# P4's bases loaded by quarters into the result tiles, and P7 begun with the two row pairs that P6 ended on

## The chip, the cores and the metric

One core of one Trainium2 chip. The metric is the device time of one execution in microseconds, the median of three runs for the kernel before.

## The reference

A soft mixture of experts: every token's output is the sum over all eight experts of that expert's matrix product, weighted by the router's softmax.

```python
batch, seq, hidden, n_experts, expert_hidden = 16, 512, 512, 8, 2048
probs = softmax(router_logits)                       # over the 8 experts
for e in range(n_experts):
    output += probs[:, :, e:e+1] * np.matmul(x, expert_weights[e])
```

As one product it is (8192 tokens) x (8 experts x 512) x (2048 columns): the left operand is x times a probability, the right operand is all the expert weights.

## The kernel before, in words

The product is cut in halves in all three directions and made by seven products instead of eight, twice over (Strassen's scheme in the form with seven products, an outer level P1 to P7 and an inner level of seven steps), and in some stages a third time. Rows are taken in 16 row pairs q; pair q has the row blocks 2q and 2q+1 of 256 tokens. Column half 0 or 1 has 1024 columns, of which a step takes 512.

An outer product r of pair q is `product(r, q)`. It has a left operand (`Left`, made by VectorE, DVE in the profile, from a block of x, a block of probabilities and for some products a kept operand), a right operand (`Right`, sums of weights), a *base* that is added to its result, and a sink that stores the result. Its seven inner steps run in the order `STEPS = (1, 5, 6, 2, 7, 3, 4)` on TensorE (PE), eight matmuls of 128x512 each. Every product gives four result tiles of 128x512 in f32, called (0,0), (1,1), (0,1) and (1,0) after row half and column half (`INNER`), 256 KB each. Steps 1, 5, 6 and 4 are the first that touch the bases (0,0), (1,1), (0,1) and (1,0); steps 2, 7, 3 and 4 are the last, after which the result is stored.

Work goes in *stages*, mostly of two products whose steps alternate. The order of the outer products is: P1 and P2, then P5 and P6 together, then eight stages of P7, eight of P4, and P3. P6's operand (its two halves `t[0]`, `t[1]`) is kept: `keep_z` stores it to `z_dram[q]`, and P7 and P3 read it back through a `ZBlock` of 1 MB. P7's base is P6's stored result, read back from the output; P4's base is P7's. P7's results are plain stores; P4's and P3's are stores that accumulate in DRAM, into (row block 2q+1, columns 0) for P4.

P4's stages are made "by thirds": `by_thirds` replaces steps 1 and 5 of both products by 14 short groups of matmuls of 128x256 (four slots), and the five other steps follow, two slots each; so a P4 stage has 14 slots, as every stage of two products has. `Thirds.make` lets DVE write four sums into one tile of the pool `w` per stage (line 538).

What sets the order: every engine runs its instructions in the order that the kernel wrote down. Loads go through SyncE's queue (`sp`, SP in the profile), weight loads through ScalarE's (ACT, which also copies results, lines 611, 624, 823 to 837), stores and casts through GpSimd's (`pool`, POOL, line 121). DVE's work beside the evacuations stands in a queue of tasks with assumed costs (`later`, `need`). `at(stage, slot, ...)` hangs a load on a slot of a stage. `start_loads` issues the loads of the stage after next.

Pools and what waits for them:

- `w`, 15 tiles of 8 KB per partition: all weights, the sums of `Thirds`, the parts of the next products' weights (`by_parts`), z loads, and the bases of the odd pair of each stage.
- `h`, 12 tiles of 2 KB per partition: results, and bases loaded one quarter at a time.
- `z`, 8 tiles: operands.

The base of an even pair is a `Base`: four loads of 256 KB into tiles of `h`. The base of an odd pair is a `WideBase`: one load of 1 MB into a tile of `w`, called `base` in the profile. In both cases the result is made in the base's own place, so a quarter's tile becomes free when its own store has landed, and the wide one when the last of its four stores has:

```python
base = self.base(tn) if first else o[tn]
if first:
    o[tn] = half() if self.apart else base
```

P6's last two stages are (P6 of 14, P5 of 15) and, alone, P6 of 15. P7 began with pairs 0 and 1; the loads for it were hung by hand on slots of those two stages, one operand in two halves (`begin_half`), and DVE's work for the second stage of P7 was held back to slot 4 (`wait_for[k7] = 4`).

Of the kernel before, what the change touches and what calls it, by code (L numbers as in the profile page):

```python
# [31 lines left out]
def kernel(  # L32
# [20 lines left out]
    NH = EH // 2  # L53
# [63 lines left out]
    def sp(o, i):  # L117
        note(nc.sync.dma_start(out=o, in_=i))
# [15 lines left out]
    def new_w():  # L134
        return wpool.tile([P, K8, NB], f16, name="w", tag="w")

    def new_u():
        return zpool.tile([P, K8, HQ], f16, name="u", tag="u", bufs=1)
# [355 lines left out]
    class ZBlock:  # L494
# [8 lines left out]
            self.t = [t[:, 0], t[:, 1]]  # L503
            sp(t, z_dram[self.q].rearrange("p (h k) t -> p h k t", h=2))

        def begin_half(self, k):
            if k == 0:
                t = new_u()
                self.t = [t, None]
            else:  # L510
                t = self.t[1] = new_w().rearrange("p k (two t) -> p (k two) t", two=2)[:, ds(0, K8)]
            sp(t, z_dram[self.q][:, ds(k * K8, K8), :])

        def finish(self):
            pass

# [145 lines left out]
            sp(t, self.source)  # L662
            self.t = {(i, n): t[:, i, n] for i in range(2) for n in range(2)}

    def base_of(q, odd):
        if q % 2:
            return WideBase(out_f[ds((2 * q + odd) * HQ, HQ), ds(NH, NH)]
                            .rearrange("(t p) (n m) -> p t n m", t=2, n=2))
        return Base(lambda tn: out_rows(q, odd, 1, tn))

    INNER = ((0, 0), (1, 1), (0, 1), (1, 0))

# [21 lines left out]
    def left_of(r, q, fresh=True):  # L694
        a, b = 2 * q, 2 * q + 1
        if r == 1:
            pt = PBlock(a, P1, xp1[q - 2][1] if q in (2, 3) else None)
            if q in (2, 3):
                xs[a] = XBlock(a, xp1[q - 2][0])
            return Left(xblock(a), pt), [xblock(a), pt]  # L700
        if r in (2, 4):
            h, pt = (a, PBlock(a, P2)) if r == 2 else (b, PBlock(b, P2))
            return Left(xblock(h), pt), [xblock(h), pt]
        if r == 5:
            pt = PBlock(b, PQ)
            return Left(xblock(b), pt), [xblock(b), pt]
        if r == 6:
            pt = PBlock(a, P1)
            return Left(xblock(a), pt, of=lefts[5, q]), [xblock(a), pt]
        h = a if r == 3 else b  # L710
        pt, kept_z = PBlock(h, P2), ZBlock(q)
        return Left(xblock(h), pt, kept=kept_z), [xblock(h), pt, kept_z]

    def kept_rows(q):
# [1 line left out]

    def product(r, q, **how):
        left, loads = left_of(r, q)
        lefts[r, q] = left
        p = None  # L720
        if r == 1:
            def sink(tn, o):
                pool(kept_rows(q)(tn), o)
            p = Product(right[1], left, sink)
        elif r == 2:
            if q >= QK:
                base = products[1, q].o.__getitem__
            else:
                base = bases[2, q] = Base(kept_rows(q))
            p = Product(right[2], left, to_out(q, 0, 0), base)  # L730
        elif r == 5:
            bases[6, q] = m1 = Base(kept_rows(q))
            m1.task = {}

            p = Product(right[5], left, to_out(q, 1, 0))
        elif r == 6:
            m1 = bases[6, q]

            def base(tn):
                need(m1.task[tn])  # L740
                return m1.t[tn]
            p = Product(right[6], left, to_out(q, 0, 1), base)
        elif r == 7:
            base = bases[7, q] = base_of(q, 0)
            p = Product(right[7], left, to_out(q, 1, 1), base)
        elif r == 4:
            base = bases[4, q] = base_of(q, 1)
            p = Product(right[4], left, to_out(q, 1, 0, accum_op=ADD), base)
        else:
            p = Product(right[3], left, to_out(q, 0, 1, accum_op=ADD), **how)  # L750
        p.loads = loads
        products[r, q] = p
        return p
# [144 lines left out]
    k6 = add(product(6, 15))  # L898
    ks = {}
    for r in (7, 4):  # L900
        for q in range(0, 16, 2):
            xs.clear()
            ks.setdefault(r, add(product(r, q), product(r, q + 1)))
    k7, k4 = ks[7], ks[4]
# [21 lines left out]
            at(*where, lambda q=q, tn=tn: joined(q, tn))  # L926
    def base_at(stage, slot, r, q, *tn):
        at(stage, slot, lambda: bases[r, q].fetch(*tn))
    for r, first in ((7, k7), (4, k4)):
        for q in range(0, 16, 2):  # L930
            k = first + q // 2
            for slot, tn in zip((1, 2, 3, 5) if k == k7 else (4, 6, 8, 10), INNER):
                base_at(k - 1, slot, r, q, tn)
            base_at(k - 1, 2 if k == k7 else 7, r, q + 1)


    def wedge(kn, e):
# [212 lines left out]
        at(k - 1, half_way, lambda keep_z=keep_z: keep_z(0))  # L1150
        at(k, 5 if q < 15 else 3, lambda keep_z=keep_z: keep_z(1))

    def load_z(stage, slot, r, q, *half):
        load = products[r, q].loads[-1]
        load.by_hook = True
        at(stage, slot, lambda: load.begin_half(*half) if half else load.begin())
    third_of = {4: {}, 3: {}}
    third_made = {4: [], 3: []}

    def make_third(stage, slot, r, p):  # L1160
        def make():
            third_of[r][p] = third_sums(right[r].w[p])
        at(stage, slot, lambda: third_made[r].append(later(2.76, make)))
    load_z(k6 - 1, 0, 7, 0)
    load_z(k6 - 1, 4, 7, 1, 0)
    load_z(k6, 0, 7, 1, 1)
    load_z(k6, 4, 7, 2)
    load_z(k6, 5, 7, 3)
    at(k6 - 1, 9, lambda: queue_left(lefts[7, 0]))
    wait_for[k7] = 4  # L1170
    make_third(k4 - 1, 7, 4, 1)
    make_third(k4 - 1, 9, 4, 5)
    load_z(k3 - 1, 0, 3, 0)
# [91 lines left out]
```

## Time and profile before

| what | value |
|---|---|
| runs | 1396.3 us median of 3 (1396.05 to 1398.36) |
| profiled execution | 1394.54 us, of which 1392.8 us are the span from the first to the last instruction |
| PE busy | 1364.2 us, 98% of the span |
| DVE busy | 1118.3 us, 80% |
| ACT, POOL busy | 227.7 us, 410.8 us |
| mean granted TensorE clock | 0.994 |
| DMA | 392.63 MB, mean 282 GB/s |

The profile's page adds up one profiled execution. Busy time is that of an engine's own instructions; the idle time before an instruction is put down to what ended it. "A <- B" in the view of waits reads: A waited for B, with the total, the number of times and the longest. In the chain of waits each row is start, duration, and what the end of the kernel hung on at that moment. In the timeline of one engine, rows that follow each other are merged, and what stands in square brackets is the idle time before the row. In the view of stretches a row has the stretch and its length, then for each engine the busy time and the number of instructions, then clock, DMA share and GB/s. Times count from the span's start.

### The profile page before, as it was taken

To read this page: it belongs to the slowest core of one execution; us is meant where nothing else is said; L and a number is where in the kernel's file an instruction comes from. 1 tells how busy PE (TensorE), PEld (TensorE's weight loads), DVE (VectorE), ACT (ScalarE), POOL (GpSimd) and SP (SyncE) were. 2 spreads that over 40 slices of the span, in tenths; PEclk is the share of its full clock that TensorE was granted. 3 is DMA by queue.
4 is the path that set the end of the run, shared out by engine and by line. 5 is a ranking of instruction groups with operands and counts; after the bars stand their busy time and mean duration, and the time that the engine had idled before them with its cause. 6 is when DMAs were issued, how large, how long until landed. Compare 5 with 4: busy or idle time off the path is not lost.

```text
span 1392.8 us, 18695 instructions
## 1 busy us (share of the span) xinstructions
PE 1364.2 (98%) x6798; PEld 664.2 (48%) x6798; DVE 1118.3 (80%) x1386; ACT 227.7 (16%) x453; POOL 410.8 (29%) x652
## 2 busy tenths in 40 slices
PE   9999999999999999999999989999999888999998
PEld 4555444444444444444444434444555454455554
DVE  7877667679789887978887778889877877988884
ACT  3232111100011111111111000000121111133331
POOL 3223233321222433333331112221333332223231
PEclk9999999999999999999999999999999999999999
DMA  9998989999899999999999999997999999999976
GB/s 185 226 241 226 218 265 239 266 281 390 263 291 284 341 329 289 330 281 316 290 313 320 409 372 394 307 350 294 327 227 275 239 293 262 330 297 255 223 105 128
DMA packets 198077, 392.63 MB, mean 282 GB/s; under 512 B 53472, under 2 KB 87520, under 8 KB 190304
## 3 DMA queue, kind: packets, MB, share of 16 engines
q0 software_dynamic: 88688, 185.12, 55.1%
q1 hardware_dynamic: 105264, 177.87, 39.7%
q10 hardware_dynamic: 4032, 28.44, 5.2%
q8 instruction: 53, 0.87, 0.2%
q14 instruction: 40, 0.33, 0.1%
HBM read 245.40 MB, written 173.21 MB: 301 GB/s over the span
## 4 chain that ended last, share of the span: by engine, by line
PE 86%; DMA 7%; issue 3%; DVE 2%; POOL 1%; ACT 0%; ACTq 0%; POOLq 0%; DVEq 0%; SPq 0%
PE ps L130 65%; PE pt L130 21%; DMA out_dram<-base 2%; DMA base<-out_dram 1%; DMA h<-out_dram 1%; POOL out_dram L121 1%; DMA w<-in_expert_weights_dram 1%; DMA xT<-x 1%; DMA w<-wd 1%; DVE z L107 1%; DVE w L107 0%; DVE h L107 0%; DVE ps L107 0%; POOL w L121 0%; POOL wd L121 0%
## 5 line engine op out<-in xcount | busy, mean ns | idle before, releaser
L130 PE MATMUL ps<-w,z 128*128 128x512 f16 (+1 forms) x3760 | 825.4, 376 | 12.6 <-DVE h L107 10.3
L130 PEld LDWEIGHTS <-z 128*128 128x128 f16 x5280 | 517.8, 98 | 601.5 <-issue 21.8
L121 POOL DMA_DIRECT2D out_dram<-h x316 | 203.5, 652 | 671.7 <-ACT h L624 282.5
L130 PE MATMUL pt<-w,z 128*128 128x512 f16 (+1 forms) x1520 | 323.0, 360 | 1.8 <-DVE ps L107 1.3
L107 DVE TENSOR_TENSOR z<-xT,pT 128x2048 f16<-128x2048 f16 x220 | 266.3, 1217 | 3.6 <-DMA xT<-xs 3.6
L107 DVE TENSOR_TENSOR h<-ps,h 128x512 f32<-128x512 f32 x226 | 154.7, 687 | 114.2 <-PE ps L130 107.3
L130 PE MATMUL ps<-w,d 128*128 128x512 f16 x880 | 202.4, 383 | 8.6 <-DVE ps L107 8.6
L130 PEld LDWEIGHTS <-d 128*128 128x128 f16 x880 | 86.6, 98 | 110.8 <-issue 12.1
L107 DVE TENSOR_TENSOR z<-z,d 128x2048 f16<-128x2048 f16 x110 | 132.3, 1217 | 0.0
L107 DVE TENSOR_TENSOR w<-w 128x1024 f16<-128x1024 f16 (+2 forms) x116 | 116.3, 1016 | 4.3 <-DMA w<-wd 2.6
L611 ACT COPY h<-ps 128x512 f32<-128x512 f32 x90 | 52.7, 586 | 363.9 <-PE ps L130 343.2
L107 DVE TENSOR_TENSOR h<-pt,h 128x512 f32<-128x512 f32 x109 | 74.9, 687 | 36.1 <-PE pt L130 28.5
L624 ACT COPY h<-ps 128x512 f32<-128x512 f32 x48 | 28.1, 586 | 356.7 <-PE ps L130 289.9
L107 DVE TENSOR_TENSOR z<-z,w 128x2048 f16<-128x2048 f16 x63 | 77.2, 1225 | 2.5 <-DMA w<-z 0.4
L107 DVE TENSOR_TENSOR d<-z 128x1024 f16<-128x1024 f16 x110 | 74.6, 684 | 0.7
L121 POOL DMA_DIRECT2D out_dram<-base x64 | 47.2, 738 | 62.7 <-DVE base L107 41.7
L121 POOL DMA_DIRECT2D wd<-w x86 | 50.1, 603 | 49.3 <-DVE w L107 29.2
L121 POOL DMA_DIRECT2D w<-in_expert_weights_dram x65 | 48.3, 754 | 49.9 <-DMA wd<-w 30.1
L107 DVE TENSOR_TENSOR ps<-ps,h 128x512 f32<-128x512 f32 (+1 forms) x68 | 42.1, 620 | 24.9 <-PE ps L130 15.7
L130 PEld LDWEIGHTS <-w 128*128 128x128 f16 x528 | 49.1, 98 | 7.8 <-DMA w<-in_x_dram 1.3
L107 DVE TENSOR_TENSOR base<-ps,base 128x512 f32<-128x512 f32 x64 | 43.8, 684 | 9.3 <-PE ps L130 9.3
L121 POOL DMA_DIRECT2D kept<-h x56 | 30.8, 550 | 68.0 <-ACT h L611 35.4
(80 smaller groups left out, 491.0 us busy)
## 6 DMA issues: line engine op xcount, KB each, us to landing
out_dram<-h POOLq DMA_DIRECT2D x316, 256.0 KB, 7.4
w<-z SPq DMA_DIRECT2D x31, 1024.0 KB, 11.9
pT<-p_dram SPq DMA_DIRECT2D x108, 256.0 KB, 9.4
w<-wd ACTq DMA_DIRECT2D x27, 1024.0 KB, 10.2
h<-kept SPq DMA_DIRECT2D x100, 256.0 KB, 7.2
wd<-w POOLq DMA_DIRECT2D x72, 256.0 KB, 8.0
xT<-x SPq DMA_DIRECT2D x71, 256.0 KB, 10.0
w<-in_expert_weights_dram POOLq DMA_DIRECT2D x35, 512.0 KB, 10.0
```

The lines of the kernel that those rows point to most:

```text
L107: dve(nc.vector.tensor_tensor(out=o, in0=a, in1=b, op=op))
L121: note(nc.gpsimd.dma_start(out=o, in_=i, **how))
L130: note(nc.tensor.matmul(ps, z, w, start=start, stop=stop, skip_group_check=True))
L611: act(nc.scalar.copy(o[TN[p]], b if p == 2 else x))
L624: act(nc.scalar.copy(o[tn], b))
```

## The change

For P4, the base of both pairs is now loaded by quarters into tiles of `h`, where the results are then made; no base of P4 lies in `w` any more. The eight quarter loads of a stage hang on slots 8, 10 and 12 of the stage before and on slot 3 of the stage itself.

P7 begins with pairs 14 and 15. Their bases are P6's results, taken from the tiles where they were made, and their kept operands are P6's operands, taken from their `z` tiles; neither is loaded. Pairs 0 to 13 follow. The hand-hung loads of operands before P7, `begin_half` and `wait_for[k7]` are gone; z loads go out with the other loads of their stage, and P7's bases for pairs 0 to 13 hang on slots 4, 6, 8, 10 and 7 of the stage before.

```diff
-    def base_of(q, odd):
+    def base_of(q):
         if q % 2:
-            return WideBase(out_f[ds((2 * q + odd) * HQ, HQ), ds(NH, NH)]
+            return WideBase(out_f[ds(2 * q * HQ, HQ), ds(NH, NH)]
                             .rearrange("(t p) (n m) -> p t n m", t=2, n=2))
-        return Base(lambda tn: out_rows(q, odd, 1, tn))
+        return Base(lambda tn: out_rows(q, 0, 1, tn))
...
-        pt, kept_z = PBlock(h, P2), ZBlock(q)
+        pt = PBlock(h, P2)
+        if r == 7 and q >= 14:
+            return Left(xblock(h), pt, kept=lefts[6, q]), [xblock(h), pt]
+        kept_z = ZBlock(q)
...
-            base = bases[7, q] = base_of(q, 0)
+            base = bases[7, q] = base_of(q) if q < 14 else products[6, q].o.__getitem__
...
-            base = bases[4, q] = base_of(q, 1)
+            base = bases[4, q] = Base(lambda tn: out_rows(q, 1, 1, tn))
...
-        for q in range(0, 16, 2):
+        for q in ((14, *range(0, 14, 2)) if r == 7 else range(0, 16, 2)):
...
-    for r, first in ((7, k7), (4, k4)):
-        for q in range(0, 16, 2):
-            k = first + q // 2
-            for slot, tn in zip((1, 2, 3, 5) if k == k7 else (4, 6, 8, 10), INNER):
-                base_at(k - 1, slot, r, q, tn)
-            base_at(k - 1, 2 if k == k7 else 7, r, q + 1)
+    for q in range(0, 14, 2):
+        k = k7 + 1 + q // 2
+        for slot, tn in zip((4, 6, 8, 10), INNER):
+            base_at(k - 1, slot, 7, q, tn)
+        base_at(k - 1, 7, 7, q + 1)
+    for q in range(16):
+        k = k4 + q // 2
+        for slot, tn in zip((8, 10, 12, 17), INNER):
+            base_at(k - 1 + slot // 14, slot % 14, 4, q, tn)
...
-    load_z(k6 - 1, 0, 7, 0)
-    load_z(k6 - 1, 4, 7, 1, 0)
-    load_z(k6, 0, 7, 1, 1)
-    load_z(k6, 4, 7, 2)
-    load_z(k6, 5, 7, 3)
-    at(k6 - 1, 9, lambda: queue_left(lefts[7, 0]))
-    wait_for[k7] = 4
+    at(k6 - 1, 5, lambda: queue_left(lefts[7, 14]))
```

More of the change, by code (lines that the diff above doesn't have):

```diff
@@ L504, in begin @@
             sp(t, z_dram[self.q].rearrange("p (h k) t -> p h k t", h=2))
[L506 to L512, printed above, removed]
         def finish(self):
@@ L1151, with load_z @@
         at(k, 5 if q < 15 else 3, lambda keep_z=keep_z: keep_z(1))
-    def load_z(stage, slot, r, q, *half):
+    def load_z(stage, slot, r, q):
         load = products[r, q].loads[-1]
         load.by_hook = True
-        at(stage, slot, lambda: load.begin_half(*half) if half else load.begin())
+        at(stage, slot, load.begin)
     third_of = {4: {}, 3: {}}
```

## The prediction

> **What bounds the kernel now.** I read the page first, then PE's waits, then the chain of waits, PE's timeline and a table of the P4 stages.
>
> ```profile
> PE 1364.2 (98%) x6798; PEld 664.2 (48%) x6798; DVE 1118.3 (80%) x1386; ACT 227.7 (16%) x453; POOL 410.8 (29%) x652
> L107 DVE TENSOR_TENSOR h<-ps,h 128x512 f32<-128x512 f32 x226 | 154.7, 687 | 114.2 <-PE ps L130 107.3
> ```
>
> ```profile
> PE ps L130 <- DVE h L107: 10.3, 4, 5.4
> PE ps L130 <- DVE ps L107: 8.6, 3, 4.0
> ```
>
> PE is the bound: 28.6 us of the 1392.8 us span are not PE's. The change leaves PE's instructions as they are, in number and shape, so all that it can win is idle time, and time in which PE runs slowly after a wait. PE's large waits are seven, all for DVE's evacuations of PSUM banks: 18.9 us. They stand in two places, the start of P7 and P4.
>
> The start of P7, first in the chain, then on PE:
>
> ```profile
> 769.03 10.01 DMA w<-wd
> 779.11 14.24 DMA h<-out_dram
> 793.37 12.35 DMA xT<-x
> 805.79 19.39 DMA base<-out_dram
> ```
>
> ```profile
> 797.53 1.89 PE L130 MATMUL ps<-w,d 128*128 128x512 f16 x8 [0.92 <-DVE ps L107]
> ...
> 820.50 1.89 PE L130 MATMUL ps<-w,d 128*128 128x512 f16 x8
> 826.05 3.46 PE L130 MATMUL ps<-w,d 128*128 128x512 f16 x8 [3.66 <-DVE ps L107]
> ```
>
> For 56 us the chain is one load after the other on SP's queue, each issued as the one before lands. The wide base that goes out at 805.79 lands 19.39 us later, at 825.18; PE wanted its evacuation at 822.4, waits 3.66 us, and then needs 3.46 us for eight matmuls that take 1.89 us elsewhere, 1.57 us more.
>
> P4, one row for each of its eight stages (stretch and length, then busy us of PE, PEld, DVE, ACT, POOL with their instructions, clock, DMA share, GB/s):
>
> ```profile
> 988.20:1011.58 23.38, 23.38 (x138) 13.29 (x137) 20.27 (x29) 4.09 (x10) 9.74 (x14) 1.00 1.10 309
> 1011.58:1036.14 24.56, 23.61 (x137) 13.31 (x136) 17.74 (x27) 4.09 (x10) 6.27 (x9) 1.00 0.93 240
> 1036.14:1060.96 24.82, 23.54 (x137) 13.30 (x136) 22.00 (x33) 4.09 (x10) 13.73 (x19) 1.00 1.09 235
> 1060.96:1092.70 31.74, 26.32 (x137) 13.91 (x136) 21.78 (x31) 4.09 (x10) 9.70 (x12) 0.89 1.00 247
> 1092.70:1116.08 23.38, 23.38 (x137) 13.31 (x136) 21.55 (x31) 4.09 (x10) 9.72 (x14) 1.00 1.10 273
> 1116.08:1144.86 28.78, 25.23 (x137) 13.74 (x136) 20.24 (x29) 4.09 (x10) 10.05 (x13) 0.94 1.08 309
> 1144.86:1168.24 23.38, 23.38 (x137) 13.33 (x136) 20.43 (x31) 4.09 (x10) 9.77 (x14) 1.00 1.08 241
> 1168.24:1199.20 30.96, 26.94 (x145) 14.53 (x144) 22.15 (x31) 3.92 (x10) 7.24 (x9) 0.94 1.02 321
> ```
>
> A stage without a wait takes 23.38 us. Stages two to seven are over that by 1.18, 1.44, 8.36, 0, 5.40 and 0: 16.38 us. Why, for the largest:
>
> ```profile
> DVE w L107 <- DMA out_dram<-base: 16.6, 2, 9.2
> ```
>
> ```profile
> 1069.19 13.71 DMA out_dram<-base
> 1086.52 6.35 PE ps L130 x16
> ```
>
> DVE stands still before it writes the sums of `Thirds` into a tile of `w`: the tile it gets was a wide base, and the last accumulating store out of it needs 13.71 us to land. DVE goes in order, so every evacuation behind it is late, and PE with it. The stage's last wait is another one: in the eighth stage a weight load for P3 waits on ACT's queue for the last store of a wide base (9.05 us), ACT's copies stand behind it, then DVE, then PE:
>
> ```profile
> 1169.50 9.05 DMA out_dram<-base
> 1180.27 19.11 PE ps L130 x80
> ```
>
> ```profile
> 1180.27 3.05 PE L130 MATMUL ps<-w,d 128*128 128x512 f16 x8 [4.02 <-DVE ps L107]
> ```
>
> 4.02 us idle and 3.05 - 1.89 = 1.16 us slow: 5.18 us.
>
> **How long stores and loads take** beside P4's work (the table of DMA issues, 985 to 1200 us; KB each, median us to landing):
>
> ```profile
> out_dram<-h POOLq DMA_DIRECT2D x34, 256.0 KB, 10.5
> out_dram<-base POOLq DMA_DIRECT2D x33, 256.0 KB, 10.1
> base<-out_dram SPq DMA_DIRECT2D x7, 1024.0 KB, 15.5
> w<-wd ACTq DMA_DIRECT2D x7, 1024.0 KB, 12.4
> h<-out_dram SPq DMA_DIRECT2D x26, 256.0 KB, 12.8
> ```
>
> Two pairs of quarters issued alone, at 1036 and 1091 us, then a store in a stage with parts of P3's weights (1052 us) and those of a calm one (1145 to 1169 us):
>
> ```profile
> h<-out_dram SPq DMA_DIRECT2D x2, 256.0 KB, 9.4
> ```
>
> ```profile
> h<-out_dram SPq DMA_DIRECT2D x2, 256.0 KB, 12.7
> ```
>
> ```profile
> out_dram<-h POOLq DMA_DIRECT2D x1, 256.0 KB, 12.4
> ```
>
> ```profile
> out_dram<-h POOLq DMA_DIRECT2D x5, 256.0 KB, 7.0
> ```
>
> The steps themselves, in the P4 stage that starts at 1144.86: step 6 of both products, then the four others:
>
> ```profile
> 1150.97 3.62 PE L130 MATMUL ps<-w,d 128*128 128x512 f16 x16
> 1154.43 13.98 PE L130 MATMUL ps<-w,z 128*128 128x512 f16 x64
> ```
>
> The first row starts 3.46 us ahead of the second: 1.73 us for a step of one product.
>
> **The start of P7, part by part.** The first stage (pairs 14, 15) loads no base and no z: 4 MB of loads leave SP's queue before it, so nothing stands between P6 and P7 but DVE's work, whose instructions are the same. The 0.92 us go. The second stage's loads (z of pairs 0, 1, xT, pT) move ahead, past P6's last loads of kept results on SP; POOL's stores keep their order. The wide base of pair 1 keeps its hook, slot 7 of the first stage, and its need, the third slot of the next stage; what it no longer has ahead of it is the backlog of the chain above. From its issue at 805.79 to PE's need at 822.4 it had 16.6 us; with the 15.5 us of the wide bases' row and 0.69 us for the evacuation that is just enough, and it is issued earlier where the queue before it is free. So the 3.66 and 1.57 us go too: 0.92 + 3.66 + 1.57 = 6.15 us. What could be late in their place: P7's results of pair 15 are written into tiles out of which P6's stores must have landed. (1,1) is the tightest, with P6's steps 3 and 4 and P7's steps 1 and 5 of two products in between, 1.73 x 2 + 3.46 x 2 = 10.4 us, less 0.69 us for the evacuation and about one for the issue. The nearest rows are P4's stores, 7.0 us where it is calm and 10.5 us at the median; I take nothing, and at worst the 2 us by which the slower one misses.
>
> **P4, part by part.** No base lies in `w`, so no sums of `Thirds` wait for an accumulating store: the 16.38 us go. What takes their place is a wait for `h`. Two products now hold eight tiles of its 12, so only two pairs of quarters of the next stage can be loaded ahead; the third, base (0,1), gets the tiles of (0,0), whose accumulating stores start in the middle of the stage. SP's in-order queue holds that load until the store has landed (behind it: xT and pT of two stages on, not urgent). The time that it has:
>
> ```profile
> 1157.24 0.88 POOL L121 DMA_DIRECT2D out_dram<-h x1 [0.48 <-ACT h L624]
> ```
>
> In the stage from 1144.86 the thirds take 6.11 us, step 6 of both products 3.46 us, and the first (0,0) is stored at 12.38 us. DVE adds base (0,1) after step 6 of the first product in the next stage, 23.38 + 6.11 + 1.73 = 31.22 us. That leaves 18.84 us for a store to land, a load to be issued (0.5 us) and to land. DVE is busy 20.77 us per stage (the eight rows' 166.16 us), so it can idle 2.61 us before the stage grows; PE itself waits later, at step 7, which needs the same bank 3.46 us after step 6 of the second product begins.
>
> Bounds per hand-over between stages (there are seven): calm, 7.0 + 0.5 + 9.4 = 16.9 us, no wait; at the medians 10.5 + 0.5 + 12.8 = 23.8 us, DVE idles 4.96 us and the stage grows by 2.35 us, 16.5 us over seven. I take the load as the mean of the two lone pairs, 11.05 us, since it is issued when SP's earlier loads have landed. In three stages, those with weight parts, the store takes 12.4 us: 23.95 us, growth 23.95 - 18.84 - 2.61 = 2.5 us each. In the other four, 7.0 + 0.5 + 11.05 = 18.55 us, nothing. Sum 7.5 us. The other quarters have more time: (1,0) follows the stores of (1,1) and is wanted only at the stage's end. Splitting moves no more bytes; SP issues 8 loads per stage where it issued 5, off the path.
>
> The eighth stage's 5.18 us: the tile that the P3 weights wait for no longer hangs on a base's store, but ACT's loads share the stretch with SP's late quarters and the first z load of P3, and a load held on ACT's queue again holds the copies behind it. Nothing in the trace prices that; I leave the 5.18 us as they are, with the whole of it as gain at one end and as much again as loss at the other.
>
> **Sum.** 1394.54 - 6.15 - 16.38 + 7.5 = 1379.5 us for the profiled execution; it was 1.76 us under the median of the runs, so 1381.3 us. With no new wait 1373.8, with all seven at the medians 1390.3; with the turnover's ends 1368.6 and 1395.5.
>
> **Rivals.** *Slower: the quarters come as late as the wide base did.* One mechanism, in P4: each (0,1) waits for a store and then for a load that takes 15.5 us, the row of the wide base. 10.5 + 0.5 + 15.5 = 26.5 us, growth 5.05 us at each of seven hand-overs, 35.4 us: 1396.3 - 22.5 + 35.4 = 1409.2 us. It decides from the point where the growth eats 22.53 us, 3.22 us per hand-over, that is store and load together over 24.2 us. For it: the medians add up to 23.3 us, and without PE's waits the same bytes must go through in less time, at a DMA share of 1.0 to 1.1 already. Against it: SP's bursts of 1.5 MB go, and the lone pairs took 9.4 and 12.7 us. Chance 0.19.
> The Trainium skill speaks against the splitting as well: "DMA: Bandwidth & Descriptors", in the section "Measured (HBM→SBUF, 128 partitions, SWDGE, issued from GpSimd)", says to batch DMAs to at least 1 MiB, and its section "Anatomy of one DMA — SWDGE (gpsimd) path" fits 2.0 us plus bytes over 436e3; an estimate from it is four times 2.6 us for the quarters against 4.4 us for the whole, 6 us per stage and some 1429 us if nothing overlapped. The trace agrees only in part: a quarter takes 12.8 us and four times as much 15.5 us, so most of either is queueing.
>
> *The start of P7 keeps its wait:* the wide base of pair 1 has the same hook and the same need, and again takes 19.39 us. 3.66 + 1.57 = 5.23 us stay: 1386.5 us. Against it: its chain began with loads that are gone. 0.07.
>
> *All waits go, the turnover's too:* 1368.6 us. For it: DVE and PE have room in every stage without a wait. 0.10.
>
> *No difference:* hand-overs at the medians, 16.5 us, and a turnover as bad again, 5.2 us: 1395.5 us or a little more. 0.06.
>
> **How the numbers follow.** Forecast (1373 to 1391 us) 0.58. What this kernel's measurement can tell is 0.2%, 2.8 us. Faster by more: 0.58 + 0.07 + 0.10 = 0.75; the same: 0.06; slower: 0.19. The range goes from 1368 us, all waits gone, to 1399 us: past the case of no difference, and into the slower rival up to a growth of 3.6 us per hand-over (1396.3 - 22.53 + 7 x 3.6), so that the most of that rival, some 0.15, is left out.
>
> **What would show it.** Right: PE without a wait from 785 to 830 us; no wait of DVE `w` for `out_dram<-base` in P4; instead DVE `h<-ps,h` waiting for `DMA h<-out_dram`, 2 to 5 us in the stages with weight parts, and P4 stages of 23.4 to 26 us. Wrong: PE's wait at the second stage of P7 stays; P4 stages of 27 us and more one after the other, with DVE waiting for quarters; or a longer stand of ACT in P4's last stage.

## The result, and the profile after

| kernel | runs | median, us | range, us |
|---|---|---|---|
| before | 4 | 1396.88 | 1396.05 to 1398.36 |
| changed | 4 | 1382.57 | 1380.78 to 1385.06 |

The ratio is 0.9898, with a 95% interval of 0.988 to 0.9916: 14.3 us less. Timed once more beside the last three experiments, the changed kernel took 1378.42 us (1377.88 to 1378.94) where the kernel before took 1395.87 us: ratio 0.987, interval 0.985 to 0.989. The profiled execution of the changed kernel took 1382.55 us, of which 1380.8 us are the span; that of before 1394.54 and 1392.8 us.

The page of the changed kernel, the engines and the group of evacuations into `h`:

```profile
PE 1361.1 (99%) x6798; PEld 662.9 (48%) x6798; DVE 1120.3 (81%) x1386; ACT 227.6 (16%) x453; POOL 410.9 (30%) x652
L107 DVE TENSOR_TENSOR h<-ps,h 128x512 f32<-128x512 f32 x269 | 182.9, 688 | 138.5 <-PE ps L130 112.5
```

PE and DVE do the same number of instructions; 43 evacuations more land in `h` (269 against 226), at a mean of 688 ns where it was 687. What PE waits for, over the whole execution:

```profile
PE ps L130 <- DVE z L107: 10.0, 4, 4.4
PE ps L130 <- DVE h L107: 1.5, 2, 1.2
PE ps L130 <- ACT ps L595: 1.2, 1, 1.2
PE pt L130 <- DVE ps L107: 0.6, 1, 0.6
```

The 18.9 us of large waits for evacuations are down to a fraction; in their place PE waits 10.0 us for operands in `z`, 3.3 us of them in P4 and 6.7 after it. In P4 that is the same queue of DVE's seen from another place: DVE makes operands and evacuates in one order, and an evacuation that stands still holds the operand behind it. After P4 a late load stands behind it as well, as is shown below.

The start of P7, in the chain of waits, where before there were 56 us of loads:

```profile
794.73 10.36 PE ps L130 x48
...
815.45 3.45 PE pt L130 x16
818.90 10.36 PE ps L130 x48
```

Nothing but PE: from 760 to 985 us it has no wait at all. 10.36 us for 48 matmuls are 1.727 us for the eight of a step.

The P4 stages (the second and the third, left out, are 23.38 us as well), and as the last row the stretch from the start of the eighth to P3's first stage of thirds (columns as before: stretch, length, busy time of PE, PEld, DVE, ACT, POOL, clock, DMA share, GB/s):

```profile
981.04:1004.42 23.38, 23.38 (x137) 13.29 (x136) 20.28 (x29) 4.09 (x10) 9.75 (x13) 1.00 1.09 265
...
1051.18:1074.56 23.38, 23.38 (x137) 13.30 (x136) 20.69 (x29) 4.09 (x10) 9.20 (x12) 1.00 1.10 268
1074.56:1100.52 25.96, 23.88 (x137) 13.12 (x136) 20.63 (x31) 4.09 (x10) 10.10 (x15) 1.00 1.10 273
1100.52:1124.02 23.50, 23.50 (x137) 13.31 (x136) 20.70 (x30) 4.09 (x10) 9.55 (x13) 1.00 1.05 258
1124.02:1151.33 27.31, 25.24 (x137) 13.65 (x136) 21.39 (x32) 4.09 (x10) 10.48 (x14) 0.94 1.09 253
1151.33:1224.05 72.72, 63.59 (x305) 30.36 (x304) 54.40 (x67) 11.97 (x24) 17.48 (x21) 0.95 1.05 333
```

The last stretch in the kernel before:

```profile
1168.24:1236.45 68.21, 61.83 (x305) 30.04 (x304) 54.58 (x67) 12.09 (x24) 17.39 (x21) 0.97 1.05 309
```

I call this stretch the *turnover*. Without a wait it would take 59.65 us: 23.38 for the eighth stage and 21 steps of P3 at 1.727. With this, the whole difference of the two profiles can be laid out:

| part | before | changed | difference |
|---|---|---|---|
| to the first P4 stage | 988.20 | 981.04 | -7.16 |
| seven P4 stages | 180.04 | 170.29 | -9.75 |
| turnover | 68.21 | 72.72 | +4.51 |
| the rest | 156.35 | 156.75 | +0.40 |
| span | 1392.8 | 1380.8 | -12.0 |

Seven P4 stages without a wait are 163.66 us, so 16.38 us of loss became 6.63. In the turnover the loss went from 8.56 to 13.07 us.

**The new waits in P4.** DVE's waits, 985 to 1200 us:

```profile
DVE h L107 <- DMA h<-out_dram: 14.7, 9, 5.7
...
DVE h L107 <- DMA wd<-w: 3.3, 2, 2.5
```

There is no line of `w` waiting for `out_dram<-base` any more; DVE waits for quarters (the longest wait, 5.7 us, comes only in the eighth stage). On DVE's timeline, in the fifth stage:

```profile
1084.66 0.69 DVE L107 TENSOR_TENSOR h<-ps,h 128x512 f32<-128x512 f32 x1 [1.69 <-DMA h<-out_dram]
1087.81 0.69 DVE L107 TENSOR_TENSOR h<-ps,h 128x512 f32<-128x512 f32 x1 [2.46 <-DMA wd<-w]
```

By the order of the loads the first wait is for a base (1,1), whose load went out at 1070.40 and took 14.1 us. The second wait is for the first base (0,1), whatever the row names. Its place came free when the store issued at 1063.56 had landed, and its load went out at 1072.10. The two rows of the table of DMA issues, for the one instant each:

```profile
out_dram<-h POOLq DMA_DIRECT2D x1, 256.0 KB, 8.5
```

```profile
h<-out_dram SPq DMA_DIRECT2D x1, 256.0 KB, 15.6
```

1072.10 + 15.6 is 1087.7, where DVE goes on. The view puts the wait down to a store of weights that ended nearby: where the named releaser has nothing to do with the instruction's operands, look for the transfer that has.

**The turnover.** In the chain of the changed kernel:

```profile
1139.28 12.22 PE ps L130 x48
...
1151.61 26.86 DMA h<-out_dram
1178.91 0.58 ACT ps L595
1179.54 3.49 PE ps L130 x16
1183.03 8.92 DMA w<-z
```

and on PE:

```profile
1187.50 3.49 PE L130 MATMUL ps<-w,z 128*128 128x512 f16 x8 [4.35 <-DVE z L107]
1199.91 2.57 PE L130 MATMUL ps<-w,z 128*128 128x512 f16 x8 [2.38 <-DVE z L107]
```

The base (1,0) of the last pairs goes out at slot 3 of the eighth stage, behind P3's first loads on SP's queue, and needs 26.86 us (and 30.34 for the second). ACT stands still behind it, SP's next z load goes out only as the second lands, and P3's operands are late. The table of DMA, queues and issues from 1150 to 1185 us, shows the company (q10 is ACT's queue, q1 SP's, q0 POOL's; packets, MB, share of 16 engines' time):

```profile
q10 hardware_dynamic: 934, 6.87, 47.2%
q0 software_dynamic: 1077, 1.96, 30.7%
q1 hardware_dynamic: 1271, 3.10, 26.8%
...
w<-wd ACTq DMA_DIRECT2D x7, 1024.0 KB, 11.5
...
h<-out_dram SPq DMA_DIRECT2D x2, 256.0 KB, 28.6
```

The engines are busy throughout, and a megabyte on ACT's queue takes 11.5 us where a quarter of one on SP's takes 28.6.

Most of the 26.86 us is a place in a queue, for the time runs from the issue. SP's queue lands what was issued before the two quarters first: the z load of 1148.84 at 1156.94, then four loads of 256 KB at 1160.62, 1165.12, 1169.58 and 1174.00, then the two quarters at 1178.47 and 1182.97. So it lands 256 KB about every 4.5 us. In the same time ACT's queue lands its loads of 1 MB at 1162.52, 1166.99, 1172.21, 1176.63 and 1181.09, one about every 4.6 us. Both have 128 rows; SP's rows are 2 KB long and ACT's 8 KB. POOL's stores of 256 KB land at the same pace.

### The profile page after: what moved, and what is told of

Its sections match the earlier page's. It is cut to its first block, busy times and chain, and to the rows that moved or that the text cites. A ratio compares the mean times of both kernels' runs of the same rounds, so it can differ in the third digit from the quotient of the medians.

```text
span 1380.8 us, 18720 instructions
## 1 busy us (share of the span) xinstructions
PE 1361.1 (99%) x6798; PEld 662.9 (48%) x6798; DVE 1120.3 (81%) x1386; ACT 227.6 (16%) x453; POOL 410.9 (30%) x652
## 4 chain that ended last, share of the span: by engine, by line
PE 90%; DMA 5%; issue 2%; POOL 1%; DVE 1%; ACT 0%; ACTq 0%; POOLq 0%; DVEq 0%
PE ps L130 67%; PE pt L130 23%; DMA h<-out_dram 2%; DMA wd<-w 1%; POOL out_dram L121 1%; DMA w<-in_expert_weights_dram 1%; DVE z L107 1%; DMA w<-z 1%; DVE w L107 0%; POOL w L121 0%; DVE h L107 0%; DVE ps L107 0%; POOL wd L121 0%; DVE d L107 0%; ACT ps L595 0%
## 5 line engine op out<-in xcount | busy, mean ns | idle before, releaser
L130 PE MATMUL ps<-w,z 128*128 128x512 f16 (+1 forms) x3760 | 824.4, 376 | 11.5 <-DVE z L107 10.0
L121 POOL DMA_DIRECT2D out_dram<-h x352 | 231.9, 684 | 681.1 <-ACT h L616 294.9
L107 DVE TENSOR_TENSOR h<-ps,h 128x512 f32<-128x512 f32 x269 | 182.9, 688 | 138.5 <-PE ps L130 112.5
L130 PE MATMUL ps<-w,d 128*128 128x512 f16 x880 | 199.3, 379 | 1.2 <-ACT ps L595 1.2
L603 ACT COPY h<-ps 128x512 f32<-128x512 f32 x90 | 52.7, 586 | 369.2 <-PE ps L130 358.3
L616 ACT COPY h<-ps 128x512 f32<-128x512 f32 x57 | 33.4, 586 | 364.4 <-PE ps L130 348.3
L107 DVE TENSOR_TENSOR z<-z,w 128x2048 f16<-128x2048 f16 x60 | 73.5, 1225 | 8.2 <-DMA w<-z 6.2
L107 DVE TENSOR_TENSOR ps<-ps,h 128x512 f32<-128x512 f32 (+1 forms) x77 | 48.4, 629 | 20.1 <-PE ps L130 15.9
L599 ACT COPY h<-ps 128x512 f32<-128x512 f32 x63 | 35.4, 600 | 74.9 <-PE ps L130 73.8
L107 DVE TENSOR_TENSOR h<-h 128x512 f32<-128x512 f32 (+2 forms) x69 | 45.2, 675 | 0.1
## 6 DMA issues: line engine op xcount, KB each, us to landing
h<-out_dram SPq DMA_DIRECT2D x96, 256.0 KB, 12.4
```

The costliest lines, as they stand in the source:

```text
L107: dve(nc.vector.tensor_tensor(out=o, in0=a, in1=b, op=op))
L121: note(nc.gpsimd.dma_start(out=o, in_=i, **how))
L130: note(nc.tensor.matmul(ps, z, w, start=start, stop=stop, skip_group_check=True))
L599: act(nc.scalar.copy(o[tn], q if p == 5 else x))
L603: act(nc.scalar.copy(o[TN[p]], b if p == 2 else x))
L616: act(nc.scalar.copy(o[tn], b))
```

## The experiments

**The two parts alone.** First the changed kernel with P4's bases as before:

```diff
-            base = bases[4, q] = Base(lambda tn: out_rows(q, 1, 1, tn))
+            if q % 2:
+                base = WideBase(out_f[ds((2 * q + 1) * HQ, HQ), ds(NH, NH)]
...
-    for q in range(16):
+    for q in range(0, 16, 2):
...
-        for slot, tn in zip((8, 10, 12, 17), INNER):
+        for slot, tn in zip((4, 6, 8, 10), INNER):
+            base_at(k - 1, slot, 4, q, tn)
+        base_at(k - 1, 7, 4, q + 1)
```

> The change's P7 part alone: P7 begins with pairs 14 and 15 from P6's tiles, P4's odd bases stay wide loads into w. My theory (two independent gains): P4 began 7.16 us earlier in the profiled execution of the changed kernel (first P4 matmul at 981.04 us instead of 988.20), so this kernel is 6 to 7.5 us faster than the kernel before, about 1389.5 us, its P4 stages again show DVE waiting before it writes the sums of Thirds, with some 16 us over 23.38 us a stage, and P3's start is as before. Rival (the two parts need each other: P4's wide bases meet more traffic when P7's end is earlier): under 3 us of gain, P4 over by more than 20 us.

Measured: 1389.5 us (1386.61 to 1392.42; before 1395.65 beside it), ratio 0.9955, interval 0.9943 to 0.9968. That is 6.15 us. P4 keeps its losses (stages of 25.3, 24.82, 31.37 and 28.38 us) and their cause:

```profile
DVE w L107 <- DMA out_dram<-base: 15.7, 2, 8.7
```

Its turnover was not as before: it took 70.39 us, 10.74 us of loss for 8.56, though no late quarter stands in it. ACT stood there for a store out of a wide base, 7.24 us, as it had for 7.7 in the kernel before.

Then the kernel before with P4's part only:

```diff
-            base = bases[4, q] = base_of(q, 1)
+            base = bases[4, q] = Base(lambda tn: out_rows(q, 1, 1, tn))
...
+    for q in range(16):
+        k = k4 + q // 2
+        for slot, tn in zip((8, 10, 12, 17), INNER):
+            base_at(k - 1 + slot // 14, slot % 14, 4, q, tn)
```

> The change's P4 part alone: P4's bases by quarters into h, P7 in the old order with its hand-hung loads. My theory: PE's waits at the start of P7 (0.92, 0.37 and 3.66 us) stay; P4's first seven stages take 9.75 us less than before, as in the changed kernel; the start of P3 costs 4 to 5 us more than before. So about 5 us faster than before, 1391.5 us. Rival (the loss at P3's start comes from P7's new order, not from the quarters): 9 to 10 us faster than before, 1387 us.

Measured: 1387.36 us (1384.83 to 1393.54), ratio 0.9949, interval 0.9931 to 0.9967: 8.3 us. That is near the rival's 1387 us and far from the theory's 1391.5, though the interval, 4.6 to 9.6 us, just holds the theory's gain as well. The profile is the theory's all the same. The seventh stage and the turnover lose 17.4 us together, as in the changed kernel, with P7 in its old order:

```profile
1128.22:1157.62 29.40, 25.40 (x137) 13.66 (x136) 22.38 (x34) 4.09 (x10) 10.55 (x14) 0.94 1.07 254
1157.62:1228.62 71.00, 62.00 (x305) 30.02 (x304) 54.23 (x67) 12.05 (x24) 17.53 (x21) 0.98 1.05 333
```

The last two quarters took 26.75 and 30.34 us here too. What made the profiled execution, 1386.74 us, shorter than the theory's time lies elsewhere: it reached P4 2.36 us sooner than that of the kernel before, by code that is the same in both. The wide base of pair 1 took 17.06 us there instead of 19.39. So single profiles differ by 2 us where nothing was changed.

The gains of the parts add up to 14.4 us; the whole change's is 14.3 us in one measurement and 17.5 in the other. Within that spread the parts don't touch each other.

**Fourteen result tiles.** The changed kernel with more room in `h`; to make it, the one tile `u` for parts of weights is taken from the pool `z`:

```diff
-    hpool = ctx.enter_context(tc.tile_pool(name="hpool", bufs=12))
+    hpool = ctx.enter_context(tc.tile_pool(name="hpool", bufs=14))
...
-        return zpool.tile([P, K8, HQ], f16, name="u", tag="u", bufs=1)
+        return new_z()
```

> The changed kernel with 14 tiles of h instead of 12; the room comes from the tile u, whose three kinds of use early in the kernel now take a tile of the pool z. My theory (what is left in P4 is a wait for h tiles: base (0,1) can't be loaded before (0,0)'s accumulating store has landed): with 14 tiles the (0,1) loads go out a third of a stage earlier, DVE's waits for h<-out_dram in the second to seventh stage of P4 go, and the 6.6 us by which these stages exceed 23.38 us go to under 2: about 1377 us. Rival (the DMA engines are full in these stages, and a load that is issued earlier only waits longer): landings of 15 us and more as before, P4 over by 5 us and more, 1381 to 1384 us. A wait early in the kernel, at the z tile taken for u, would be its own cost and is read apart.

Measured: 1383.03 us (1380.68 to 1385.7), ratio 0.9912, interval 0.9898 to 0.9925. The first and the sixth P4 stage, then the seventh and the turnover:

```profile
981.79:1005.84 24.05, 23.55 (x138) 13.31 (x137) 20.28 (x29) 3.93 (x10) 9.75 (x14) 1.00 1.10 296
...
1099.35:1122.73 23.38, 23.38 (x137) 13.29 (x136) 20.92 (x29) 4.09 (x10) 11.20 (x14) 1.00 1.08 250
```

```profile
1122.73:1146.11 23.38, 23.38 (x137) 13.33 (x136) 20.06 (x31) 4.09 (x10) 9.17 (x13) 1.00 1.09 280
1146.11:1222.46 76.35, 63.58 (x306) 30.64 (x304) 54.28 (x67) 12.05 (x24) 17.54 (x21) 0.96 1.05 323
```

The five stages after the first are without a wait, so the new waits in P4 do come from too few places for quarters. (`u` is used six times, from 155 to 277 us, far from P4.) But the turnover grew by 3.6 us, its two quarters took 29.64 and 32.08 us, and no time was won: what P4 gained the turnover lost.

**Does the size of a load count?** The kernel with P7's part alone, the odd base of P4 now as four loads of 256 KB into the same wide tile of `w`:

```diff
+    class SplitBase(Base):
+        def fetch(self):
+            t = wpool.tile([P, 4, NB], f32, name="base", tag="w").rearrange("p (t n) m -> p t n m", t=2)
+            self.t = {(i, n): t[:, i, n] for i in range(2) for n in range(2)}
+            for tn in INNER:
+                sp(self.t[tn], self.source(tn))
```

> As the kernel with the P7 part alone, but P4's odd base is loaded by four loads of 256 KB into the same wide tile of w. It tells the size of the loads apart from the place of the results. My theory (size is of no account, the tile that the results hold is): within 1.5 us of the kernel with the P7 part alone, about 1389.5 us, and DVE's waits for w tiles stay. By the Trainium skill's rule of large DMAs (DMA: Bandwidth & Descriptors, section Measured) it would be slower, by an estimate up to 6 us a stage, if the four loads did not overlap; rival from rows (quarters are what cures P4, as they come in time): 8 to 10 us faster than the kernel with the P7 part alone.

Measured: 1388.5 us (1385.77 to 1390.45), ratio 0.9948, interval 0.9936 to 0.9961, against 1389.5 with one load. Splitting neither costs nor gains what can be told apart by the time; waits stay where the tile stays:

```profile
DVE w L107 <- DMA out_dram<-h: 7.9, 1, 7.9
DVE w L107 <- DMA out_dram<-base: 5.8, 1, 5.8
```

(The wait of the first row ended at 1073.1 us; a store out of a wide base landed at 1072.9.) P4 lost 10.4 us in this profile, against 16.4 in that of P7's part alone, and the turnover 13.7 against 10.7. One execution of each doesn't tell whether splitting by itself takes something off P4's waits.

**Moving the transfers of the turnover.** Four edits of the changed kernel. The (1,0) quarters of the last stage ahead of P3's loads:

```diff
-        for slot, tn in zip((8, 10, 12, 17), INNER):
+        for slot, tn in zip((8, 10, 12, 17 if q < 14 else 13), INNER):
```

> The changed kernel whole; only the two (1,0)-quarter base loads of the last P4 stage are queued four slots sooner, ahead of P3's first x, p and z loads in SyncE's queue and ahead of ScalarE's seven 1 MB weight loads. In the changed kernel these two 256 KB loads took 26.86 and 30.34 us, the last P4 results waited for them, and from P4's last stage to P3's first stage of thirds 72.72 us went by where 59.65 us is matmul time. Theory (they are late because they stand behind P3's loads and beside ScalarE's weights): they land in 10 to 14 us, the waits of 4.35 and 2.38 us at the start of P3 go, and of the 13 us of loss 4 to 7 us go: 1376 to 1379 us. Rival (the sixteen DMA engines are full there, and whatever is queued later is late instead): the quarters are in time, but P3's z and x loads behind them are late by as much, the loss stays 11 to 13 us: 1381 to 1383 us.

Measured: 1382.87 us (1376.83 to 1388.48; before 1397.19), ratio 0.9895, interval 0.9869 to 0.9921. The profiled execution was the slowest of the six, 5.6 us over the median. The quarters were in time:

```profile
h<-out_dram SPq DMA_DIRECT2D x2, 256.0 KB, 7.3
```

and PE now waited for weights instead:

```profile
PE pt L130 <- DMA w<-wd: 4.1, 1, 4.1
PE ps L130 <- DMA w<-wd: 2.8, 1, 2.8
```

The rival was right that something else would be late; it named z and x, and it was the weights. The turnover took 73.05 us, and the seventh stage 31.13. P3's weights sooner:

```diff
-    turnover(k3 - 1, (1, 2, 5, 6, 7, 8, 11), 3, "b22")
+    turnover(k3 - 2, (8, 12, 15, 18, 20, 22, 25), 3, "b22")
```

> The changed kernel whole; only P3's seven weight loads are queued sooner on ScalarE, the first two by 7 and 4 slots (into the stage before), the others by 1 to 4 slots. Theory (the crowd at 1150 to 1185 us makes the loss): spread out, the weights are through sooner, the (1,0) quarters take 18 to 25 us, the loss falls by 2 to 5 us, and the last stages of P4 lose at most 1 us by quarters that now have weights beside them: 1378 to 1381 us. Rival (the bytes only move, and meet P4's own quarters, for which matmuls wait sooner than for P3's): the eighth and the seventh stage of P4 grow by 3 us or more: 1383 to 1386 us.

Measured: 1378.27 us (1377.49 to 1383.62), ratio 0.9871, interval 0.9853 to 0.989: by itself the theory's number. Whether it is a gain over the changed kernel is taken up below. The weights in rows of 2 KB, each megabyte as two loads of 512 KB:

```diff
-        note(nc.scalar.dma_start(out=t, in_=stored[what, kn]))
...
+            cut = "p (x y c) n -> p y x (c n)"
+            for y in range(2):
+                note(nc.scalar.dma_start(out=t.rearrange(cut, x=2, y=2)[:, y], in_=src.rearrange(cut, x=2, y=2)[:, y]))
```

> The changed kernel whole; only ScalarE's seven 1 MB weight loads for P3 are each cut into two loads of 512 KB whose rows are 2 KB long instead of 8 KB. Bytes, order and queues stay. Theory (the queues take turns packet by packet, so that 8 KB packets get some four times the bytes of the 2 KB packets of SyncE's loads): with equal packets the two (1,0) quarters land in 14 to 20 us instead of 26.86 and 30.34, the weights take 15 us and more instead of 9 to 11.5 for a megabyte, and the loss at the change from P4 to P3 falls by 3 to 6 us: 1377 to 1380 us. Rival (the quarters are late by their place in SyncE's queue and by the sum of bytes alone): they still take 25 to 30 us, and the time stays 1381 to 1384 us.

Measured: 1395.91 us (1391.7 to 1398.55), ratio 0.9989, interval 0.9977 to 1.0001: the whole gain gone. The queues from 1150 to 1185 us, then the two quarters:

```profile
q10 hardware_dynamic: 2458, 4.75, 36.9%
q1 hardware_dynamic: 1421, 4.17, 35.0%
q0 software_dynamic: 1111, 2.02, 33.5%
```

```profile
h<-out_dram SPq DMA_DIRECT2D x2, 256.0 KB, 16.4
```

The theory's mechanism held: with short rows ACT moved 4.75 MB instead of 6.87, SP 4.17 instead of 3.10, and the quarters came in 16.4 us instead of 28.6; SP's loads of 256 KB landed every 1.3 to 2.7 us where it had been 4.5. Its time did not: the weights, which had been quick because the quarters were slow, were late in their turn (PE waited 10.8 us for them, and the turnover took 83.81 us). Fourteen tiles, quarters first and weights sooner together:

> The changed kernel with the three edits together: fourteen result tiles instead of twelve (P4's stages then run without a wait), the (1,0) quarters of the last P4 stage queued ahead of P3's loads, and P3's weight loads queued sooner. Theory (the result tiles explain P4's 6.6 us of waits, and the crowded turnover the rest): both gains add, P4's stages 23.4 us each and the change to P3 64 to 69 us: 1371 to 1377 us. Rival (what one wait loses the next one takes, as with fourteen tiles alone): the loss at the change to P3 is 12 us or more whatever stands before it: 1381 to 1384 us.

Measured: 1380.51 us (1379.65 to 1383.72), ratio 0.9888, interval 0.9872 to 0.9905, between theory and rival. The gains don't add: in the profiled execution, the slowest of the five, the turnover took 76.90 us, PE waiting 10.5 us in one piece for a copy of ACT's.

**The changed kernel again, with the edit that looked best.**

> The changed kernel as it is, as the measure for the three beside it. All theories: 1381 to 1384 us.

Measured: 1378.42 us, given above, and under the 1381 to 1384 that every theory had set for it. The profile has the seventh stage and the turnover 3.2 us shorter than the first one of the same kernel:

```profile
1123.64:1149.05 25.41, 23.55 (x137) 13.22 (x136) 21.16 (x32) 4.09 (x10) 10.35 (x14) 1.00 1.11 270
1149.05:1220.46 71.41, 63.35 (x306) 30.62 (x305) 54.20 (x67) 12.07 (x24) 17.52 (x21) 0.95 1.06 334
```

> The changed kernel with P3's weight loads queued sooner (the first two by 7 and 4 slots), once more beside the changed kernel itself. If its 1378.27 us was a gain over the changed kernel: 1377 to 1380 us, 3 us or more under it. If it was the spread between calls: within 1.5 us of it.

Measured: 1380.34 us (1375.8 to 1381.35), ratio 0.9876, interval 0.9852 to 0.9899. Beside the changed kernel it is no better; what looked like 4 us was spread. No version here is shown to beat the changed kernel.

**Less traffic.** P4's last sixteen stores left out:

```diff
-            p = Product(right[4], left, to_out(q, 1, 0, accum_op=ADD), base)
+            p = Product(right[4], left, to_out(q, 1, 0, accum_op=ADD) if q < 12 else lambda tn, o: None, base)
```

> The changed kernel without P4's last sixteen accumulating stores of 256 KB (those of row pairs 12 to 15, which GpSimd queued between 1139 and 1185 us); their rows keep what stood there before. Loads, their order and the queues stay. Theory (at 1150 to 1185 us the sixteen DMA engines are full, and any transfer taken away there lets the late ones come sooner): the two (1,0) quarters, 26.86 and 30.34 us before, land in 12 to 20 us, the way from P4's last stage to P3's first thirds takes 62 to 68 us instead of 72.72, and the time is 1370 to 1378 us. Rival (the quarters are late by their place behind SyncE's other loads and by waits on earlier landings, whatever else is under way): 25 us and more, 71 us and more, 1381 to 1384 us.

Measured: 1374.84 us (1369.71 to 1375.91), ratio 0.9838, interval 0.9813 to 0.9862, 3.6 us under the changed kernel beside it. The two quarters, then the seventh stage and the turnover:

```profile
h<-out_dram SPq DMA_DIRECT2D x2, 256.0 KB, 9.1
```

```profile
1123.69:1152.64 28.95, 25.24 (x138) 13.67 (x136) 21.83 (x32) 4.09 (x10) 4.78 (x7) 0.94 1.02 310
1152.64:1216.33 63.69, 61.50 (x306) 30.07 (x305) 54.40 (x67) 12.24 (x24) 9.24 (x11) 0.97 0.97 311
```

With 4 MB less the quarters are quick in their old place in the queue, quicker than the theory's 12 to 20 us, and the turnover is down to 63.69 us, as the theory had it. Against the changed kernel beside it half of that came back in the seventh stage, 28.95 us for 25.41. But the run does more than take bytes away. A tile that isn't stored is free as soon as it is made, so SP's queue ran ahead. The loads of the two quarters, then the first load of P3's weights:

```profile
1145.05 2.12 SPq L118 DMA_DIRECT2D h<-out_dram  x2
...
1154.72 0.33 ACTq L164 DMA_DIRECT2D w<-wd  x1
```

The quarters went out 7.5 us sooner than in the changed kernel beside it (1152.55), and the second had landed at 1155.39, as the weights only began, so they were all but through ahead of them. Fewer bytes and an earlier issue are not told apart here.

And the same stores as plain ones, so that what they should be added to is overwritten:

```diff
+            p = Product(right[4], left, to_out(q, 1, 0, **({'accum_op': ADD} if q < 12 else {})), base)
```

> The changed kernel with P4's last sixteen stores (row pairs 12 to 15) as plain stores of the same 256 KB instead of accumulating ones; what they should be added to is overwritten. Theory A (an accumulating store costs the engines well over its bytes): most of what the kernel without these stores gains comes here too, 1372 to 1379 us. Theory B (it costs them its 256 KB like any other): the time of the changed kernel, 1381 to 1384 us.

Measured: 1378.13 us (1376.67 to 1379.78), ratio 0.9869, interval 0.9847 to 0.989. The number lies in theory A's range, but it is the time of the changed kernel beside it, 1378.42, and so theory B's case. POOL's queue from 1150 to 1185 us, here and in the changed kernel beside it:

```profile
q0 software_dynamic: 766, 2.53, 20.5%
```

```profile
q0 software_dynamic: 1006, 1.83, 30.7%
```

The engines' time says otherwise: 0.205 x 35 / 2.53 = 2.8 us of all sixteen engines for a megabyte, against 0.307 x 35 / 1.83 = 5.9 us. By the packet there is little between them, 0.205 x 35 x 16 / 766 = 0.15 us of one engine against 0.307 x 35 x 16 / 1006 = 0.17, but a plain packet carried 3.3 KB on average and an accumulating one 1.8 KB. The lighter stores did bring the quarters sooner (13.3 us) and the turnover down to 66.58 us, but the seventh stage took 30.47 us. Why it did, with less in its way, is not settled.

The loss in the seventh stage and the turnover together (their lengths less 83.03 us), with the time of the profiled execution that it is read from and the median of its runs:

| kernel | loss, us | profiled, us | median, us |
|---|---|---|---|
| before | 8.6 | 1394.54 | 1396.88 |
| P7's part alone | 10.7 | 1389.75 | 1389.5 |
| base split in `w` | 14.0 | 1386.49 | 1388.5 |
| P4's part alone | 17.4 | 1386.74 | 1387.36 |
| changed | 17.0, 13.8 | 1382.55, 1378.94 | 1382.57, 1378.42 |
| weights sooner | 12.8, 15.3 | 1379.28, 1381.35 | 1378.27, 1380.34 |
| fourteen tiles | 16.7 | 1380.68 | 1383.03 |
| quarters first | 21.2 | 1388.48 | 1382.87 |
| all three | 19.5 | 1383.72 | 1380.51 |
| rows of 2 KB | 31.3 | 1396.82 | 1395.91 |
| stores plain | 14.0 | 1379.78 | 1378.13 |
| stores left out | 9.6 | 1374.82 | 1374.84 |

Two profiles of one kernel differ by some 3 us, so rows that are nearer than that say nothing of each other. The second and the third row have no late quarters, and lose no less than the kernel before all the same.

## Why the prediction was right, and where it was off

The forecast was 1381.3 us, the result 1382.57 (1378.42 in the second measurement). For the profiled execution it was 1379.5, and it took 1382.55. By its own steps:

*The start of P7, 6.15 us gone.* Shown: P7's part alone won 6.15 us (4.5 to 8.0 by its interval), and PE has no wait from 760 to 985 us. The profile gives 7.16 us. That the median has the forecast's very digits is luck, with 2 us between executions at this place. The wide base of pair 1 went out at 798.27 and took 12.6 us, so the rival in which its wait stays fell, and the results of pair 15 waited for no store. One reading was loose: the first row of the chain of 56 us, `w<-wd`, is a weight load on ACT's queue; the three others are SP's.

*P4's 16.38 us gone, 7.5 us of new waits.* The first half is shown on both sides: the waits for `out_dram<-base` stay where the wide bases stay, and go with them. The new waits came to 6.63 us (4.70 in the second profile, in the fourth, fifth and seventh), in two stages with weight parts, the fifth and the seventh, by 2.58 and 3.93 us where 2.5 each was worked out for three; the third, which has such parts too, lost nothing, and the sixth 0.12. The other stages lost nothing. The hand-over of the fifth stage took 8.5 us for the store and 15.6 for the load, 24.1 us; the sum in the prediction was 12.4, 0.5 and 11.05, 23.95 us. That it comes out is luck, because two errors met: the store was quicker and the load was not a lone one. In the seventh stage the same hand-over took 9.5 us and 12.0, 21.5 us, which by the sum costs nothing worth naming, and the stage still grew by 3.93: PE was idle for 2.07 us, and its matmuls took 25.24 us for 23.38, slow after the wait. The prediction had put that slow time into the start of P7 and left it out here. So the size of 7.5 us is right in sum and not stage by stage. That it is the room in `h` that makes DVE wait, the run with fourteen tiles shows.

*The slower rival* had the load's price almost exactly (15.5 us) and was still wrong: its point, 24.2 us or a growth of 3.22 us, was meant for every hand-over. The fifth stage's came to 24.1 us, and the seventh stage grew by 3.93, but three of the first seven stages, the second to the fourth, lost nothing. So the margin was thin in two of the three stages with weight parts, and enough elsewhere. The Trainium skill's rule of batching to 1 MiB ("DMA: Bandwidth & Descriptors", section "Measured (HBM→SBUF, 128 partitions, SWDGE, issued from GpSimd)") is not borne out for these loads, which go through SP's queue and beside others: four loads in the place of one made 1388.5 us against 1389.5.

*The turnover, 5.18 us left as they were.* This is the term that was mis-sized. The place where PE had lost 5.18 us is clean, but the loss from there to P3's thirds rose from 8.56 to 13.07 us (11.76 in the second profile), near the end of +5.2 us that was set. The mechanism stood in the prediction, ACT's weights beside SP's late quarters and P3's first z load. What it lacked was a price, and it had one sentence wrong: that (1,0) has more time. In the last stage its load goes out behind P3's loads and beside seven megabytes of weights, and took 26.86 and 30.34 us. That these two come with P4's part and hold ACT and DVE is shown; that they make the whole growth is not. The wait that they replace, ACT's for a store out of a wide base, went on in P7's part alone, and its turnover lost 10.74 us too.

Summed for the profiled execution: 1.0 us better up to P4, 0.9 better in P4, 4.5 worse at the turnover and 0.4 in the rest are the 3.05 us by which 1379.5 was too low.

What bounds the turnover: the sixteen engines are full, and what is queued there is late in one order or another. Quarters first made weights late, short rows made weights late, and more room in P4 made the turnover longer; sixteen stores less won 3.6 us, by fewer bytes or by an earlier issue. A full share alone does not mark such a stretch: it is 1.05 in the turnover and 1.05 to 1.11 in P4, where most of the waits that the change took away stayed away. Order and rows both move the quarters: 7.3 us (4.35 and 10.34) ahead of P3's loads, 16.4 with short rows beside them, 28.6 in the changed kernel. The Trainium skill says in "DMA: Bandwidth & Descriptors", section "Queues, rings and completion order", that each engine takes turns between the queues, a packet at a time. The changed kernel looks like that: 128 rows about every 4.5 us on SP's queue and on ACT's, and 934, 1077 and 1271 packets of the three queues, with 6.87, 1.96 and 3.10 MB in them. With short rows the counts were 2458, 1111 and 1421, so turns of equal count are not what the profile's packets show.

Left open: why the changed kernel took 1382.57 us in one measurement and 1378.42 in another, when the kernel before took 1396.88 and 1395.87 beside it. The two profiles differ mostly in the seventh stage and the turnover, where the engines are full; what tips them was not tried.

## What to carry to other kernels

Where results are made in the place of their bases, a tile is busy from the load of the base until the landing of the store; whoever shares such tiles with other work makes that work wait for stores. Give the bases to the pool that turns over fastest, and count its tiles by store plus load plus issue against the time that one stage gives, with the slow matmuls after a wait added. Before an edit that moves loads, write down what each queue holds in that stretch, in its order: in the turnover a wait that was taken away came back under another name in five edits, and none is shown to beat the changed kernel. Leaving sixteen stores out won 3.6 us, which a kernel that must give the whole result cannot do, and stores that took the engines half the time for a megabyte won nothing. And profile a kernel more than once before 3 us are given a cause.

## What was not expected of the hardware

Side by side, SP's queue landed a load of 256 KB with rows of 2 KB about every 4.5 us, and ACT's a load of 1 MB with rows of 8 KB about every 4.6 us. So the short rows got a quarter of the bytes, and a quarter behind five other loads took 26.86 us, the next one 30.34. With rows of 2 KB on both sides they took 16.4 us. Accumulating stores took some 5.9 us of all sixteen engines for a megabyte, plain ones on the same queue some 2.8 us, worked out above from the queue's share, with other traffic beside both; the packets cost about the same, and the plain ones were larger. And still the time of the kernel was the same with either.
